# A two-layer decoder trunk on one core: the steps of a large and a small expert in a new order

## The chip, the cores and the metric

The kernel runs on one core of a Trainium2 chip. The metric is the device time of one execution in microseconds (us). Before the change the median of three runs is 1153.97 us (1151.48 to 1154.01).

## The reference, cut to what matters

The program computes two decoder layers on 256 tokens of width 1024, in float32. The change touches the last stage only, a mixture of experts: a router picks two of eight experts for each token, and each expert is a SwiGLU network with 2816 hidden columns.

```
logits = h @ router                       # (256, 8)
top_val, top_idx = top_k(logits, 2)
gates = scatter(softmax(top_val))         # (256, 8), two per row
for e in range(8):
    y = (silu(h @ w_gate[e]) * (h @ w_up[e])) @ w_down[e]
    out = out + gates[:, e:e+1] * y
x = x + out
```

The weights of one expert are three matrices of 1024 x 2816 float32. Over eight experts that is 277 MB, which all comes from HBM once.

## The kernel before, in words

**Experts as large and small.** The router's result sorts the experts by their number of tokens (expert 0 is always put first). Four are "large", with up to 128 token slots, four "small", with up to 64 (`BIG`, `HALFP`). A token reaches its slot by a matmul with a one-hot matrix (`gather_split`, `gather_all`), and an expert's output y goes back to the residual x3 by a matmul with the transposed one-hot (`scatter`, line 1508), whose results VectorE adds with the gate.

**Chunks and units.** Each expert is done in 11 chunks (`FC`) of 256 hidden columns. The weights of a chunk are three units of 1 MB (128 x 2048 float32): the first and the second half of the gate and up product (here gu0 and gu1) and the down product (dn). A chunk takes gu0, gu1, then SiLU and product (`ff_act`, `sm_act`: ScalarE, then VectorE), transposes on TensorE (`ff_tr`, two for a large chunk, `sm_tr`, one for a small), a copy out of PSUM, and dn. Eight experts have 264 units.

**Large work.** For a large expert every operand is the sum of a high and a low part in fp32r: ScalarE writes the high part (`wh`), VectorE the low part (`wl`, line 332 by the helper's line), and `mm3` (lines 515 to 518) multiplies three times. A large unit is 12 matmuls with 128 columns of weights. After the transposes ScalarE writes the high part of the hidden values and VectorE the low part.

**Small work.** A small expert multiplies the float32 unit as it was loaded. Its 64 token slots fill half of the array's columns, so two products run side by side, in the column groups 0 to 63 and 64 to 127 (`sm_gu`, `sm_dn`, lines 1532 and 1555).

**The stream of units.** `Stream` (line 692) loads the units in the order of use with DMAs on SyncE's queue (SP, line 442), each into the next free buffer. There are nine buffers in the long run: five `raw`, one `xres`, one of `xg`, `more` and `fl`. A large unit's buffer is free when its split is done (`make`), a small unit's when its matmuls are done (`done`); the load of the next unit is issued at that place of the program, and SP waits there until the buffer is really free. `ahead(n)` splits the next large unit if fewer than n stand split; there are four pairs of split tiles (`HL`).

**The order before.** `items` alternates large and small chunks, with the small ones four chunks late (`LAG`), so that there are 40 cycles of both, four large chunks alone ahead of them and four small ones behind. Each item runs its gu0, the transposes of the item before, its gu1, and the dn of the item before. A cycle, with L the large and S the small chunk (S' and L' the one before), is thus on TensorE:

```
gu0 L | tr S' | gu1 L | dn S' | gu0 S | tr L | gu1 S | dn L
```

A split is asked for after tr S', after tr L and after gu1 S. What is due once in 11 cycles stands behind the dn: the scatter of the finished expert (`pend`), y's split, one-hots, their transposes, and gathers of later experts. `manual_schedule` keeps each engine's instructions in program order. This part of the program is not ordered by the recorder and its costs, which stop at line 1602.

Of the kernel before, what the change touches and what calls it, by code (L numbers as in the profile page):

```python
# [19 lines left out]
P = 128  # L20
EPS = 1e-6
NEG = -1e30
FC = 11
# [26 lines left out]
HL = 4  # L50
# [3 lines left out]
BIG = 4  # L54
HALFP = 64
LAG = 4
# [337 lines left out]
def kernel(ctx: ExitStack, tc: tile.TileContext, a, out: bass.AP):  # L394
# [32 lines left out]
    def pa():  # L427
        return rec.tile(psp, [P, 512], F32, "ps", 8, name="ps")
# [337 lines left out]
    def ff_gu(st, xs, gu, u, ahead=True):  # L766
        wh, wl = st.next(ahead)
        for b in range(len(xs)):
            for kk in range(4):
                k = 4 * u + kk  # L770
                mm3(gu[b], xs[b][0][:, k, :], xs[b][1][:, k, :], wh[:, kk * 512:(kk + 1) * 512],
                    wl[:, kk * 512:(kk + 1) * 512], k == 0, k == 7)

    def ff_act(gu, scales=None, act=None):
        hs = []
        for b in range(len(gu)):
            si = tw(256)
            hh = tw(256)
            if scales:
                tact(si, gu[b][:, 0:256], AF.Silu, scale=scales[b])  # L780
                V.scalar_tensor_tensor(hh, gu[b][:, 256:512], scales[b], si, op0=OP.mult, op1=OP.mult)
            else:
                (act or tact)(si, gu[b][:, 0:256], AF.Silu)
                V.tensor_tensor(hh, gu[b][:, 256:512], si, OP.mult)
            hs.append(hh)
        return hs

    def ff_tr(hs):
        n = 2 * len(hs) * P
        tp = pa()  # L790
        transposes([h[:, i * P:(i + 1) * P] for i in range(2) for h in hs], tp)
        th, tl = tw(n, dt=F32R), tw(n, dt=F32R)
        S.activation(th, tp[:, :n], AF.Copy)
        V.tensor_tensor(tl, tp[:, :n], th.bitcast(F32), OP.subtract)
        return th, tl

    def ff_dn(st, t, yps, first, last, ahead=True):
        wh, wl = st.next(ahead)
        nb = len(yps)
        order = [(b, i, hf) for b in range(nb) for i in range(2) for hf in range(2)]  # L800
        for b, i, hf in sorted(order, key=lambda o: o[2]) if last else order:
            rec.late = HALF if last and hf else 0
            sl = slice((i * nb + b) * P, (i * nb + b + 1) * P)
            ws = slice(i * 1024 + hf * 512, i * 1024 + (hf + 1) * 512)
            mm3(yps[b][hf], t[0][:, sl], t[1][:, sl], wh[:, ws], wl[:, ws], first and i == 0, last and i == 1)
# [53 lines left out]
    for g in range(2):  # L859
        ps = [pa() for i in range(2)]  # L860
        for u in range(2):
            wh, wl = split(raw0[u]) if g == 0 else unit(a["w0"][2 + u])
            for c in range(4):
                o = ps[c // 2][:, (c % 2) * 256:(c % 2) * 256 + 256]
# [8 lines left out]
        for c in range(4):  # L873
            j = 4 * g + c
# [624 lines left out]
    def y_split(yps):  # L1499
        rec.late = 0  # L1500
        y = [(tw(dt=F32R), tw(dt=F32R)) for i in range(2)]
        for i in range(2):
            rec.late = HALF if i else 0
            S.activation(y[i][0], yps[i], AF.Copy)
            V.tensor_tensor(y[i][1], yps[i], y[i][0].bitcast(F32), OP.subtract)
        return y

    def scatter(t, y, g, acc, store=False):
        for i in range(2):
            rec.late = HALF if i else 0  # L1510
            cs = slice(i * 512, (i + 1) * 512)
            for b in range(2):
                sp = pa()
                T.matmul(sp, t[:, b * P:(b + 1) * P], y[i][0], start=True, stop=False)
                T.matmul(sp, t[:, b * P:(b + 1) * P], y[i][1], start=False, stop=True)
                V.scalar_tensor_tensor(acc[:, b, cs], sp, g(b), acc[:, b, cs], op0=OP.mult, op1=OP.add)
                if store:
                    dma(ov[:, b, cs], acc[:, b, cs])
        rec.late = 0
# [5 lines left out]
    def large_split(src):  # L1525
        x = large_tile()
        S.activation(x[0], src, AF.Copy)
        V.tensor_tensor(x[1], src, x[0].bitcast(F32), OP.subtract)
        return x


    def sm_gu(xs, gu, u):
        w = st.next(False)
        for kk in range(4):
            k = 4 * u + kk
            wv = w[:, kk * 512:(kk + 1) * 512].rearrange("p (g f) -> p g f", g=2)
            for i in range(2):
                mmx(gu[i * HALFP:(i + 1) * HALFP, 0:256].rearrange("p (g f) -> p g f", g=2), xs[:, k],
                    wv[:, :, i * P:(i + 1) * P], k == 0, k == 7)
        st.done()  # L1540

    def sm_act(gu):
        si, hh = tw(P), tw(P)
        tact(si, gu[:, 0:P], AF.Silu)
        V.tensor_tensor(hh, gu[:, P:256], si, OP.mult)
        return hh

    def sm_tr(hh):
        tp = pa()
        transposes([hh], tp)  # L1550
        t = tw(P)
        S.activation(t, tp[:, 0:P], AF.Copy)
        return t
# [14 lines left out]
        return lambda: gtile([P, 2048], F32, n, 2) if n == "xres" else mo([P, 2048], n)  # L1568


    items = []
    for g in range(BIG * FC + LAG):
        if g < BIG * FC:
            items.append((False, *divmod(g, FC)))
        if g >= LAG:
            items.append((True, *divmod(g - LAG, FC)))
    regs = {}

    def source(r, j):

        if r == 0:
            return a["moe"][j]

        def at_run():
            if r not in regs:
                regs[r] = nc.values_load(ids[0:1, r:r + 1], engines=[mybir.EngineType.SP], min_val=0, max_val=7)
            return a["moe"][bass.ds(regs[r] * (3 * FC) + j, 1)].rearrange("u p c -> p (u c)")
        return at_run

    srcs, whole = [], []  # L1590
    for i in range(len(items) + 1):
        for it, js in ((items[i] if i < len(items) else None, (0, 1)), (items[i - 1] if i else None, (2,))):
            for j in js if it else ():
                srcs.append(source(it[1] + (BIG if it[0] else 0), 3 * it[2] + j))
                whole.append(it[0])
    st = Stream(srcs, ([(place("xres"), 999), (place("xg0"), XG)],
                       [(place("xg1"), 999), (place("more"), 999), (place("fl"), 999)]), whole)
    xb = large_tile()
# [6 lines left out]
    xs = top([P, BIG, 8, HALFP], "xs")  # L1605
    oh_s = one_hots(BIG, BIG, HALFP)
    ov = out.rearrange("(b p) d -> p b d", p=P)
    ys, ohs, ohts, hs, pend = {}, {}, {}, {}, None
    N = len(items)
    for i in range(N + 1):  # L1610
        it = items[i] if i < N else None
        was = items[i - 1] if i else None
        alone = not (it and was and it[0] != was[0])
        if it:
            sm, p, c = it
            gu = pa()
            xsp = xs[:, p] if sm else [xb]
            sm_gu(xsp, gu, 0) if sm else ff_gu(st, xsp, [gu], 0, False)
        if was:
            t = sm_tr(hs[was]) if was[0] else ff_tr(hs[was])  # L1620
        st.ahead(HL if alone or it[0] else HL - 1)
        if it:
            sm_gu(xsp, gu, 1) if sm else ff_gu(st, xsp, [gu], 1, False)
            hs[it] = sm_act(gu) if sm else ff_act([gu])
            if not sm and c == FC - 1 and p < BIG - 1:
                xb = large_split(xl[:, p % 2])
        if alone or it[0]:
            st.ahead(HL)
        if was:
            wsm, wp, wc = was  # L1630
            if wc == 0:
                ys[wsm] = [pa(), pa()]
            (sm_dn if wsm else lambda t, y, *f: ff_dn(st, t, [y], *f, False))(t, ys[wsm], wc == 0, wc == FC - 1)
            if alone:
                st.ahead(HL)
        if pend:
            scatter(*pend)
            pend = None
        if was and was[2] == FC - 1:
            r = was[1] + (BIG if was[0] else 0)  # L1640
            pend = (ohts[was[0]], y_split(ys[was[0]]), lambda b, r=r: gateo[:, b, r:r + 1], x3, i == N)
        if not it:
            continue
        if c == 0:
            ohs[sm] = both_halves(BIG + p) if sm else one_hots(p, 1)[:, :, 0]
        if c == 1:
            ohts[sm] = oht_of(ohs[sm][:, 0], ohs[sm][:, 1])
        if sm:
            continue
        if p == 0 and c < LAG:  # L1650
            for k in range(2 * c, 2 * c + 2):
                gather_all(k, oh_s, xs)
        if p == 0 and LAG + 2 <= c < LAG + 6:
            if c == LAG + 2:
                xl, oh_l = mo([P, 2, 8, P], "xg0"), one_hots(1, 2)
            for k in range(2 * (c - LAG - 2), 2 * (c - LAG - 1)):
                gather_all(k, oh_l, xl)
        if p == 1 and 2 <= c < 6:
            if c == 2:
                oh_l = one_hots(3, 1)  # L1660
            for k in range(2 * c - 4, 2 * c - 2):
                gather_all(k, oh_l, xl[:, 0:1])
    scatter(*pend)
    man.close()


# [177 lines left out]
```

## Time and profile before

| what | value |
|---|---|
| median of three runs | 1153.97 us |
| profiled execution | 1151.45 us, span of its instructions 1149.7 us |
| TensorE busy | 1121.7 us (98%) |
| VectorE busy | 713.0 us (62%) |
| ScalarE busy | 588.5 us (51%) |
| read from HBM | 345.95 MB, 302 GB/s over the span |
| mean granted TensorE clock | 0.995 |

The span is the time from the first to the last instruction of the profiled execution. Busy times of TensorE are modelled at the ends of matmuls, so a busy TensorE need not be one at its best pace: the starts of instructions are read here, not their durations. The expert stage goes from about 467 us to the end.

### The profile page before, as it was taken

How to read it: one execution, taken by the hardware profiler on the slowest of the kernel's cores; microseconds unless marked ns; L12 is line 12 of the kernel's file. 1: busy time of each engine (PE TensorE's matmuls, PEld its weight loads, DVE VectorE, ACT ScalarE, POOL GpSimd, SP SyncE). 2: the span in 40 equal slices, each digit the busy share in tenths (PEclk: the TensorE clock that was granted, in tenths of full speed). 3: DMA queues.
4: the chain of work that ended last, by engine and by line, in shares of the span. 5: the costliest groups of instructions: out<-in, count | busy, mean ns of one | idle time of the engine just before them, and what ended most of it. 6: DMA issues, size and time to landing. Idle time of an engine off the chain costs nothing.

```text
span 1149.7 us, 16360 instructions
## 1 busy us (share of the span) xinstructions
PE 1121.7 (98%) x6091; PEld 825.0 (72%) x6091; DVE 713.0 (62%) x1170; ACT 588.5 (51%) x987; POOL 29.0 (3%) x59
## 2 busy tenths in 40 slices
PE   6999999999999999999999999999999999999997
PEld 6888888888877877786766667666666666666663
DVE  5989955445388877785456455557556556565531
ACT  5868744434378656573545444444454444444421
POOL 1040000000300000000000000000000000000000
PEclk9999999999999999899999999999999999999999
DMA  9551565556334515389999999999999999999994
GB/s 351 186 200 74 183 219 184 183 183 202 135 135 181 220 37 186 145 308 376 374 406 419 394 412 384 396 423 422 421 422 421 422 422 420 421 423 419 423 420 161
DMA packets 52070, 348.14 MB, mean 303 GB/s; under 512 B 5904, under 2 KB 6032, under 8 KB 11536
## 3 DMA queue, kind: packets, MB, share of 16 engines
q1 hardware_dynamic: 51984, 347.02, 76.1%
q8 instruction: 50, 0.82, 0.3%
q14 instruction: 36, 0.29, 0.1%
HBM read 345.95 MB, written 1.05 MB: 302 GB/s over the span
## 4 chain that ended last, share of the span: by engine, by line
PE 68%; DMA 19%; DVE 7%; ACT 4%; issue 1%; SPq 0%; ACTq 0%; DVEq 0%
DMA xres<-in_moe_dram 18%; PE ps L516 15%; PE ps L518 15%; PE ps L517 15%; PE ps L332 14%; PE ps L327 10%; DVE wl L332 4%; ACT wh L332 4%; DMA raw<-in_w_dram 1%; DVE wl L327 1%; DVE xres L332 0%; DVE tw L327 0%; DVE tw L332 0%; SPq L446 0%; DVE more L327 0%
## 5 line engine op out<-in xcount | busy, mean ns | idle before, releaser
L332 DVE TENSOR_TENSOR wl<-raw,wh 128x2048 fp32r<-128x2048 f32 x89 | 204.1, 2294 | 153.9 <-ACT wh L332 153.4
L516 PE MATMUL ps<-wh,fh 128*128 128x512 f32 (+2 forms) x720 | 290.3, 403 | 0.0
L517 PE MATMUL ps<-wl,fh 128*128 128x512 f32 (+2 forms) x720 | 279.7, 388 | 0.0
L332 ACT ACTIVATE tw<-ps 128x128 f32<-128x128 f32 (+2 forms) x202 | 72.9, 363 | 320.1 <-PE ps L332 288.6
L332 ACT ACTIVATE wh<-raw 128x2048 fp32r<-128x2048 f32 x89 | 169.9, 1909 | 60.4 <-PE ps L518 56.5
L516 PEld LDWEIGHTS ps<-wh,fh 128*128 128x128 f32 x720 | 135.9, 189 | 28.1
L517 PEld LDWEIGHTS ps<-wl,fh 128*128 128x128 f32 x720 | 136.0, 189 | 23.9
L332 DVE TENSOR_TENSOR tw<-ps,tw 128x256 f32<-128x256 f32 (+3 forms) x158 | 66.7, 427 | 137.1 <-ACT tw L332 136.9
L518 PE MATMUL ps<-wh,fl 128*128 128x512 f32 (+2 forms) x368 | 142.1, 386 | 0.0
L518 PE MATMUL ps<-wh,fh 128*128 128x512 f32 x352 | 138.3, 393 | 0.0
L332 DVE TENSOR_TENSOR wl<-xres,wh 128x2048 fp32r<-128x2048 f32 x39 | 89.2, 2288 | 46.1 <-ACT wh L332 46.1
L332 PE MATMUL ps<-raw,xs 128*64 128x256 f32 x960 | 116.3, 384 | 0.0
L516 PE MATMUL ps<-wh,tw 128*128 128x512 f32 (+1 forms) x276 | 113.7, 412 | 0.7 <-ACT tw L327 0.7
L518 PE MATMUL ps<-wh,tw 128*128 128x512 f32 (+1 forms) x276 | 108.9, 395 | 0.0
L517 PE MATMUL ps<-wl,tw 128*128 128x512 f32 (+1 forms) x276 | 108.7, 394 | 0.0
L332 ACT ACTIVATE wh<-xres 128x2048 fp32r<-128x2048 f32 x39 | 74.8, 1918 | 55.6 <-DMA xres<-in_moe_dram 53.2
L327 DVE TENSOR_TENSOR wl<-raw,wh 128x512 fp32r<-128x512 f32 (+1 forms) x149 | 98.3, 680 | 2.4 <-ACT wh L327 2.4
L332 PEld LDWEIGHTS ps<-raw,xs 128*64 128x64 f32 x960 | 64.8, 137 | 41.3 <-issue 14.5
L327 ACT ACTIVATE wh<-raw 128x512 fp32r<-128x512 f32 (+1 forms) x131 | 75.3, 627 | 16.8 <-PE ps L518 13.2
L518 PEld LDWEIGHTS ps<-wh,fl 128*128 128x128 f32 x368 | 69.1, 188 | 14.6 <-DVE fl L327 0.5
L518 PEld LDWEIGHTS ps<-wh,fh 128*128 128x128 f32 x352 | 66.3, 188 | 14.5
L516 PEld LDWEIGHTS ps<-wh,tw 128*128 128x128 f32 x276 | 51.9, 188 | 26.6 <-issue 15.4
(280 smaller groups left out, 1332.3 us busy)
## 6 DMA issues: line engine op xcount, KB each, us to landing
raw<-in_moe_dram SPq DMA_DIRECT2D x142, 1024.0 KB, 9.4
xres<-in_moe_dram SPq DMA_DIRECT2D x41, 1024.0 KB, 10.5
raw<-in_ffn_dram SPq DMA_DIRECT2D x30, 1024.0 KB, 4.8
xg<-in_moe_dram SPq DMA_DIRECT2D x27, 1024.0 KB, 9.3
more<-in_moe_dram SPq DMA_DIRECT2D x26, 1024.0 KB, 10.8
fl<-in_moe_dram SPq DMA_DIRECT2D x25, 1024.0 KB, 9.7
raw<-in_w_dram SPq DMA_DIRECT2D x23, 1024.0 KB, 4.9
raw<-in_ffn_dram SPq DMA_DIRECT2D x12, 256.0 KB, 3.8
```

The lines of the kernel that those rows point to most:

```text
L327: return (self.name, self.cost(fn, args, kw), lambda: real(*args, **kw))
L332: return getattr(self.eng, fn)(*args, **kw)
L516: nc.tensor.matmul(ps, xh, wh, start=start, stop=False)
L517: nc.tensor.matmul(ps, xh, wl, start=False, stop=False)
L518: nc.tensor.matmul(ps, xl, wh, start=False, stop=stop)
```

## The change

The alternating items become a list of steps. Each step is one unit's matmuls (`gu0`, `gu1`, `dn`), the transposes of a chunk (`tr`), the scatters that are due (`late`), or the rest (one-hots, their transposes, gathers). A full cycle is now, with l0 and s0 the chunks before:

```
tr l0 | gu0 l | late | tr s0 | dn l0 | gu1 l | rest | dn s0 | gu0 s | gu1 s
```

The units are loaded in the order of these steps. After each `tr` and each `dn` the stream is asked for a split up to four. An expert's scatter, which stood behind the next dn, now comes in the next cycle's `late`. The one-hots of an expert are made after its first gu1 and transposed five steps later or at the first `rest` from then on.

```diff
-    items = []
-    for g in range(BIG * FC + LAG):
-        if g < BIG * FC:
-            items.append((False, *divmod(g, FC)))
-        if g >= LAG:
-            items.append((True, *divmod(g - LAG, FC)))
+    def chunk(sm, g):
+        return (sm, *divmod(g, FC)) if 0 <= g < BIG * FC else None
+
+    steps = []
+    for g in range(BIG * FC + LAG + 1):
+        l, l0, s, s0 = chunk(False, g), chunk(False, g - 1), chunk(True, g - LAG), chunk(True, g - LAG - 1)
+        if l and s0:
+            o = [("tr", l0), ("gu0", l), ("late", None), ("tr", s0), ("dn", l0), ("gu1", l), ("rest", l),
+                 ("dn", s0), ("gu0", s), ("gu1", s)]
+        elif l0:
+            o = [("gu0", l), ("tr", l0), ("gu0", s if not l else None), ("tr", s0), ("gu1", l), ("more", l), ("dn", l0),
+                 ("late" if l else "", None), ("rest", l), ("dn", s0), ("gu0", s if l else None), ("gu1", s)]
+        else:
+            o = [("gu0", l or s), ("tr", s0), ("gu1", l or s), ("more", l), ("dn", s0), ("late", None), ("rest", l)]
+        steps += [(k, it) for k, it in o if it or k == "late"]
...
+    unit_of = {"gu0": 0, "gu1": 1, "dn": 2}
+    used = [(k, it) for k, it in steps if k in unit_of]
+    srcs = [source(it[1] + (BIG if it[0] else 0), 3 * it[2] + unit_of[k]) for k, it in used]
+    whole = [it[0] for k, it in used]
...
-    for i in range(N + 1):
-        it = items[i] if i < N else None
-        was = items[i - 1] if i else None
-        alone = not (it and was and it[0] != was[0])
...
+    for n, (k, it) in enumerate(steps):
+        if k == "late":
+            while pend:
+                scatter(*pend.pop(0))
+            continue
+        sm, p, c = it
+        if k == "more":
+            st.ahead(HL)
+        elif k in ("gu0", "gu1"):
+            if k == "gu0":
+                gu[sm] = pa()
+            if sm:
+                sm_gu(xs[:, p], gu[sm], unit_of[k])
+            else:
+                ff_gu(st, [xb], [gu[sm]], unit_of[k], False)
+            if k == "gu1":
+                hs[sm] = sm_act(gu[sm]) if sm else ff_act([gu[sm]])
+                if not sm and c == FC - 1 and p < BIG - 1:
+                    xb = large_split(xl[:, p % 2])
+                if c == 0:
+                    ohs[sm] = n, both_halves(BIG + p) if sm else one_hots(p, 1)[:, :, 0]
+        elif k == "tr":
+            ts[sm] = sm_tr(hs[sm]) if sm else ff_tr(hs[sm])
+            st.ahead(HL)
+        elif k == "dn":
+            if c == 0:
+                ys[sm] = [pa(), pa()]
+            if sm:
+                sm_dn(ts[sm], ys[sm], c == 0, c == FC - 1)
+            else:
+                ff_dn(st, ts[sm], [ys[sm]], c == 0, c == FC - 1, False)
+            st.ahead(HL)
+            if c == FC - 1:
+                r = p + (BIG if sm else 0)
+                pend.append((ohts[sm], y_split(ys[sm]), lambda b, r=r: gateo[:, b, r:r + 1], x3, n == len(steps) - 2))
+        else:
+            for e in list(ohs):
+                if n >= ohs[e][0] + 5:
+                    o = ohs.pop(e)[1]
+                    ohts[e] = oht_of(o[:, 0], o[:, 1])
...
```

The gathers in the last branch are the ones of before, with the same conditions.

## Rows read from the trace of the kernel before

**Rows 1.** The page, busy time, share of the span and instructions of each engine.
```profile
PE 1121.7 (98%) x6091; PEld 825.0 (72%) x6091; DVE 713.0 (62%) x1170; ACT 588.5 (51%) x987; POOL 29.0 (3%) x59
```

**Rows 2.** The page, the chain that ended last, shares of the span by line.
```profile
DMA xres<-in_moe_dram 18%; PE ps L516 15%; PE ps L518 15%; PE ps L517 15%; PE ps L332 14%; PE ps L327 10%; DVE wl L332 4%; ACT wh L332 4%; DMA raw<-in_w_dram 1%; DVE wl L327 1%; DVE xres L332 0%; DVE tw L327 0%; DVE tw L332 0%; SPq L446 0%; DVE more L327 0%
```

**Rows 3.** Windows of the expert stage: busy us, clock, DMA share, GB/s.
```profile
515.00:740.00 225.00, 223.88 (x1236) 149.38 (x1235) 122.19 (x112) 104.35 (x123) 0.00 (x0) 1.00 0.98 392
740.00:1110.00 370.00, 369.83 (x2014) 246.74 (x2013) 213.19 (x188) 169.96 (x183) 0.00 (x0) 1.00 1.01 421
```

**Rows 4.** Waits of TensorE and ScalarE from 740 us: total, times, longest.
```profile
PE ps L332 <- DVE tw L332: 0.2, 1, 0.2
...
ACT wh L332 <- DMA xres<-in_moe_dram: 53.2, 23, 4.0
```

**Rows 5.** Timeline of TensorE, one bare cycle: start, us, engine, line, tiles.
```profile
821.90 1.94 PE L332 MATMUL ps<-raw,tw 128*64 128x512 f32 x8
823.66 1.90 PE L332 MATMUL ps<-xg,xs 128*64 128x256 f32 x16
825.49 0.44 PE L332 MATMUL ps<-cp,tw 128*128 128x128 f32 x2
825.86 1.95 PE L332 MATMUL ps<-raw,xs 128*64 128x256 f32 x16
827.74 0.50 PE L516 MATMUL ps<-wh,tw 128*128 128x512 f32 x1
...
830.65 0.39 PE L516 MATMUL ps<-wh,fh 128*128 128x512 f32 x1
...
836.34 1.94 PE L332 MATMUL ps<-more,tw 128*64 128x512 f32 x8
...
842.18 0.50 PE L516 MATMUL ps<-wh,tw 128*128 128x512 f32 x1
```

**Rows 6.** Timeline of TensorE, two transposes inside 128-column work.
```profile
709.61 0.39 PE L517 MATMUL ps<-wl,tw 128*128 128x512 f32 x1
...
711.94 0.40 PE L518 MATMUL ps<-wh,tw 128*128 128x512 f32 x1
712.17 0.38 PE L332 MATMUL ps<-cp,tw 128*128 128x128 f32 x2
712.31 0.47 PE L516 MATMUL ps<-wh,fh 128*128 128x512 f32 x1
712.62 0.39 PE L517 MATMUL ps<-wl,fh 128*128 128x512 f32 x1
```

**Rows 7.** The chain in order of time: start, us, what.
```profile
755.08 1.93 ACT wh L332
```

**Rows 8.** Timelines of ScalarE and VectorE, [idle before, its releaser].
```profile
829.70 1.92 ACT L332 ACTIVATE wh<-xres 128x2048 fp32r<-128x2048 f32 x1 [1.39 <-DMA xres<-in_moe_dram]
...
1079.01 0.42 DVE L332 TENSOR_TENSOR tw<-ps,tw 128x256 fp32r<-128x256 f32 x1 [2.45 <-ACT tw L332]
...
1083.02 0.28 DVE L332 TENSOR_TENSOR tw<-ps,tw 128x128 f32<-128x128 f32 x1
...
1084.18 1.92 ACT L332 ACTIVATE wh<-xres 128x2048 fp32r<-128x2048 f32 x1 [3.24 <-DMA xres<-in_moe_dram]
...
1086.13 2.29 DVE L332 TENSOR_TENSOR wl<-xres,wh 128x2048 fp32r<-128x2048 f32 x1 [2.83 <-ACT wh L332]
```

**Rows 9.** Timeline of TensorE, small down products on both sides of a cycle with gathers.
```profile
702.24 1.94 PE L332 MATMUL ps<-xg,tw 128*64 128x512 f32 x8
...
718.12 1.94 PE L332 MATMUL ps<-fl,tw 128*64 128x512 f32 x8
```

**Rows 10.** DMA issues in 712 to 732 us: KB each, median us to landing.
```profile
more<-in_moe_dram SPq DMA_DIRECT2D x1, 1024.0 KB, 4.7
```

**Rows 11.** Timeline of TensorE, the last large and the last small down product.
```profile
1109.18 0.50 PE L516 MATMUL ps<-wh,tw 128*128 128x512 f32 x1
...
1137.54 1.94 PE L332 MATMUL ps<-xg,tw 128*64 128x512 f32 x8 [0.37 <-ACT tw L332]
```

More of the change, by code (lines that the diff above doesn't have):

```diff
@@ L1588, in source @@
         return at_run
[L1590 to L1595, printed above, removed]
+    unit_of = {"gu0": 0, "gu1": 1, "dn": 2}
+    used = [(k, it) for k, it in steps if k in unit_of]
+    srcs = [source(it[1] + (BIG if it[0] else 0), 3 * it[2] + unit_of[k]) for k, it in used]
+    whole = [it[0] for k, it in used]
     st = Stream(srcs, ([(place("xres"), 999), (place("xg0"), XG)],
@@ L1607 @@
     ov = out.rearrange("(b p) d -> p b d", p=P)
-    ys, ohs, ohts, hs, pend = {}, {}, {}, {}, None
-    N = len(items)
-    for i in range(N + 1):
-        it = items[i] if i < N else None
-        was = items[i - 1] if i else None
-        alone = not (it and was and it[0] != was[0])
[L1614 to L1627, printed above, removed]
-            st.ahead(HL)
[L1629 to L1662, printed above, removed]
@@ L1663 @@
-    scatter(*pend)
+    gu, hs, ts, ys, ohs, ohts, pend = {}, {}, {}, {}, {}, {}, []
+    for n, (k, it) in enumerate(steps):
[5 more added lines that the diff above has]
+        if k == "more":
+            st.ahead(HL)
+        elif k in ("gu0", "gu1"):
[30 more added lines that the diff above has]
+                    ohts[e] = oht_of(o[:, 0], o[:, 1])
+            if p == 0 and c < LAG:
+                for j in range(2 * c, 2 * c + 2):
+                    gather_all(j, oh_s, xs)
+            if p == 0 and LAG + 2 <= c < LAG + 6:
+                if c == LAG + 2:
+                    xl, oh_l = mo([P, 2, 8, P], "xg0"), one_hots(1, 2)
+                for j in range(2 * (c - LAG - 2), 2 * (c - LAG - 1)):
+                    gather_all(j, oh_l, xl)
+            if p == 1 and 2 <= c < 6:
+                if c == 2:
+                    oh_l = one_hots(3, 1)
+                for j in range(2 * c - 4, 2 * c - 2):
+                    gather_all(j, oh_l, xl[:, 0:1])
```

## The prediction

> **What bounds the kernel now.** I read first the page's shares of busy time [rows 1], then the chain that ended last, by line [rows 2], then two windows of the expert stage [rows 3], then the waits in it [rows 4], and last the timelines of single cycles. The reader is to see two candidates that are both full. TensorE is busy 98% of the span, and in 740 to 1110 us 369.83 of 370 us; in that stage it waits for others 0.2 us in all [rows 1, 3, 4]. The DMA engines are full as well: share 1.01 and 421 GB/s in 740 to 1110, against 0.98 and 392 GB/s in 515 to 740 [rows 3]. The line with most of the chain is a transfer, the load of an expert unit into xres, 18% [rows 2], and ScalarE waits 53.2 us for just these loads [rows 4].
>
> So the stage has two paces. TensorE's: a bare cycle (a large and a small chunk, six units) goes from the small down product at 821.90 to the next at 836.34, 14.44 us [rows 5]. The DMA's: the split of xres starts at 755.08 and at 1084.18, each time on a landing, 22 cycles apart [rows 7, 8]; 329.10 / 22 = 14.96 us, and six units of 1,048,576 bytes in 14.96 us are again 421 GB/s. Cycles with gathers or scatters take TensorE longer, 15.88 us for the one from 702.24 to 718.12 [rows 9]. Up to about 740 us TensorE sets the pace and the DMA waits for free buffers; from there on the DMA has no time left, and TensorE lives on its lead: ScalarE's wait before the xres split, 1.39 us at 829.70, has grown to 3.24 us at 1084.18 [rows 8].
>
> **The change, part by part.**
> (1) *Switches on TensorE.* Before, the two transposes of the large chunk stand between the halves of the small gate and up product. First half 823.66 to 825.49 = 1.83, the transposes to 825.86 = 0.37, second half to 827.74 = 1.88; then the large down product to 830.65 = 2.91 [rows 5]. Inside 128-column work, two transposes and one of the matmuls round them cost 712.62 - 711.94 = 0.68 for two steps of 0.23 and the transposes, so these cost 0.22; and ten steps of a large down product take 711.94 - 709.61 = 2.33, so its twelve without an entry 2.79, and the entry is 2.91 - 2.79 = 0.12 [rows 6]. After, the small block is its down product as before (1.76), the first half 1.76 (an estimate: as the down product, which too is followed by small work), the second half, with its exit, 1.85 (between 1.83 and 1.88). The transposes open the large block, 0.22 + 0.12 = 0.34, and the large down product costs 2.79. Before 1.83 + 0.37 + 1.88 + 2.91 = 6.99; after 1.76 + 1.85 + 0.34 + 2.79 = 6.74. The saving is 0.25 us, a bare cycle 14.19. Bounds: 0.15, if only the transposes gain, and 0.40, with both halves at 1.76 and no entry. I take the sum of the nearest rows, 0.25. For 40 cycles this is 10.0 us, if TensorE alone decided.
>
> (2) *Splits and lead.* In both kernels up to four large units stand split; ScalarE (1.92) and then VectorE (2.29) split each [rows 8], and both work in program order. After the change a split comes behind gu0 L (A), behind dn L (B) and behind dn S (C). Put gu0 L at 0: trS is done at 2.85, dn L 5.64, gu1 L 8.5, dn S 10.25, gu0 S 12.0, gu1 S 13.85, trL 14.19. (Cycles are numbered by their large chunk, 0 to 43; gu0, gu1 and dn are a chunk's three units, tr its transposes.) C splits the gu0 L of the cycle after next, so the 13th unit from the cycle's first must have landed. Behind C in program order stand the small chunk's SiLU and product (0.28 on VectorE) and the large chunk's high and low halves (low 0.42) [rows 8]. If the unit lands at D, the next dn L starts no sooner than D + 1.92 + 2.29 + 0.28 + 0.42 + 0.2 (an estimate for five hops; the one from ScalarE at 1086.10 to VectorE at 1086.13 is 0.03) = D + 5.1. The unit itself is used 14.19 - 2.85 = 11.34 later, so it must land 16.4 us ahead of its use. Before, only a copy and the next split stand behind the late split of xres, and the unit split at 829.70 is used at 842.18 [rows 5, 8], 12.5 us on: TensorE could run closer behind the DMA than the new order lets it.
>
> (3) *Where the DMA then is.* Nine buffers are always held. Releases in a new cycle, from its start: A 2.73 + 4.21 = 6.95, B 9.85, dn S 10.25, C 13.1 (8.5 + 0.4 for the large SiLU, an estimate by the 0.42 above, + 4.21); gu0 S and gu1 S stand behind C on SP's queue, 13.1 and 13.85. The unit that C needs is issued at gu1 S of the cycle before. Take cycle 17, the first bare one after many with extras. Before, its gu0 L starts at 712.31 [rows 6]; the dn L ahead of it, 2.91, now comes behind it, and the blocks of 13 small chunks have gained 13 x 0.25 = 3.25: it starts at 706.15. Cycle 16 lasts 15.88 - 0.25 = 15.63, so its A releases at 697.47. A load that finds the queue empty lands in 4.7 us [rows 10]: 702.17. B's, 2.9 later, lands at 705.07, and the other four at 14.96 / 6 = 2.49 each: 715.03. From here the DMA is never out of work: A of cycle 17 releases at 713.1, and its data flow 4.7 - 2.49 = 2.2 later, about when the last load is done. So 24 cycles on, the same unit of cycle 41 lands at 715.03 + 24 x 14.96 = 1074.1. It is the 245th of 264 in the order of loads; before, the 245th landed at 1084.18 [rows 8].
>
> (4) *The end.* dn L in cycle 42 starts at 1074.1 + 5.1 = 1079.2. Nothing large is left for C, so two cycles run at TensorE's pace: 1079.2 + 14.19 + 14.19 - 2.85 = 1104.7. Then the last trL (0.34) and the work that before went from the last dn L at 1109.18 to the last dn S at 1137.54, 28.36 [rows 11]: that one starts at 1133.4. What follows (y's split, scatter, store) is the same. Gain 4.1 us; with the bounds of (1), over 13 + 3 cycles, 2.5 and 6.5.
>
> (5) *Put at nothing.* The first four large chunks keep their order. Gathers, one-hots, scatters are the same instructions behind other steps; the one-hots' transposes come five steps later, a whole expert ahead of their scatter. A scatter's accumulations now stand on VectorE ahead of A, whose unit has over 20 us to its use. If that cover is gone, each of the six boundaries before cycle 41 costs some 2 us, of which TensorE wins back 14.96 - 14.19 = 0.77 a cycle.
>
> **The sum.** The profiled execution took 1151.45 (span 1149.7); less 4.1 it is 1147.35. It stands 2.5 under the median of the runs, 1153.97, so the forecast for the median is 1153.97 - 4.1 = 1149.9.
>
> **Rivals.**
> *TensorE decides alone.* The transfers keep up and 40 x 0.25 - 0.34 = 9.7 us are won: 1144.3. For it: TensorE's 0.2 us of waits. Against: the rate stayed at 421 GB/s with a share of 1.01 through 370 us [rows 3]; bare cycles of 14.19, or 14.71 with at most 14.96 - 14.44 = 0.52 for boundaries, want 443 to 428 GB/s. [...] The long windows of this trace stop at 421.
> *The lead eats the gain.* The work at boundaries (y's split, that of the next large input) goes through the same two queues as the chain to D + 5.1. If it adds some 3 us to it at the last boundary before cycle 42, about 1 us is left: 1153. For it: the chain has no slack once the DMA leads. Against: five cycles lie between that boundary and cycle 42.
> *Bursts starve the DMA (slower).* While the DMA sets the pace, SP stands at C and then issues three loads at once, at D + 4.2. From D on three units are left in the queue, 7.5 us; the new data flow from D + 4.2 + 2.2 = D + 6.4. The slack is 1.1 us. Against: that is enough by the rows. For: before, releases came more evenly, so no row shows the rate with so short a queue. From 4.1 / 24 = 0.17 us of lost DMA time in a cycle on the change is slower; at 0.4 us it is 9.6 - 4.1 = 5.5 us slower: 1159.5.
> *It doesn't do what it says*: the switches cost the same wherever they stand. Then (3) starts 3.25 later and the gain is under 1 us: 1153, counted with the second rival.
>
> **How the numbers follow.** Forecast 0.50 (own range 1147 to 1152), TensorE alone 0.17, gain eaten 0.18, starved 0.15. A measurement of this kernel can tell some 0.3%, 3.5 us, from no change. Of the forecast's 0.50, 0.30 lies beyond that and 0.20 within. Faster 0.30 + 0.17 = 0.47; same 0.20 + 0.18 = 0.38; slower 0.15. The range begins a little below the first rival and ends on the way into the starved case: 1143 to 1157.
>
> **What would show it.** (1): bare cycles of 14.2 us where TensorE still leads the pace, transposes at 0.3, no step between the small halves. (2), (3): from about 750 us on TensorE waits some 0.7 us a cycle for VectorE's large low half or small product, ScalarE waits for loads more than 53 us, and the rate is 421 GB/s from 700 us on. (4): the last small down product at about 1133, its load long landed. Wrong if TensorE still never waits (the end then comes near 1144), or if the rate in 740 to 1070 falls below 418 GB/s.

## The result and the profile after

The changed kernel is slower: 1170.44 us (median of 5 runs, 1169.43 to 1175.09) against 1153.06 for the kernel before in the same session, a ratio of 1.0164 with a 95% interval of 1.0150 to 1.0178. The forecast was 1149.9. The execution read below took 1169.43, span 1167.7.

Read in the order of the prediction. First the page: busy time of TensorE, then the chain that ended last, by line.

```profile
PE 1115.0 (95%) x6091; PEld 832.0 (71%) x6091; DVE 711.0 (61%) x1170; ACT 591.5 (51%) x987; POOL 29.0 (2%) x59
...
PE ps L332 21%; PE ps L516 17%; PE ps L517 17%; PE ps L518 17%; PE ps L327 10%; DMA raw<-in_moe_dram 5%; ACT wh L332 2%; DMA xres<-in_moe_dram 2%; DVE wl L332 2%; DVE tw L332 1%; DMA raw<-in_w_dram 1%; DVE wl L327 1%; DVE tw L327 0%; DVE xres L332 0%; SPq L446 0%
```

TensorE has less to do, 1115.0 us against 1121.7 [rows 1], and still the span is 18.0 us longer: it waits now. The windows of the expert stage, with the columns of [rows 3] (busy us of five engines, clock, DMA share, GB/s), say that the loads slowed down too, where they had been the limit: 411 GB/s for 421.

```profile
515.00:740.00 225.00, 218.56 (x1232) 152.55 (x1232) 126.00 (x113) 108.65 (x122) 0.00 (x0) 0.98 0.98 398
...
740.00:1110.00 370.00, 353.29 (x1941) 240.51 (x1940) 206.38 (x182) 167.40 (x178) 0.00 (x0) 1.00 1.00 411
```

The waits in the same 370 us (total, times, longest) name what stands in front of TensorE, for 0.2 us before [rows 4]:

```profile
ACT wh L332 <- DMA raw<-in_moe_dram: 66.0, 15, 5.5
...
PE ps L332 <- DVE tw L332: 16.5, 18, 1.9
```

One cycle in time, on SP's queue, ScalarE, VectorE and TensorE (start, us, engine, line, tiles, [idle before, releaser]). C's unit lands and ScalarE starts at 739.05; VectorE's half of the split and the small product follow; the small transposes wait for that.

```profile
736.12 0.33 SPq L442 DMA_DIRECT2D xg<-in_moe_dram  x1
743.32 0.33 SPq L442 DMA_DIRECT2D fl<-in_moe_dram  x1
743.90 7.41 SPq L442 DMA_DIRECT2D raw<-in_moe_dram  x4
...
739.05 1.92 ACT L332 ACTIVATE wh<-fl 128x2048 fp32r<-128x2048 f32 x1 [4.62 <-DMA fl<-in_moe_dram]
...
741.00 2.29 DVE L332 TENSOR_TENSOR wl<-fl,wh 128x2048 fp32r<-128x2048 f32 x1 [5.12 <-ACT wh L332]
743.21 0.61 DVE L332 TENSOR_TENSOR tw<-ps,tw 128x128 f32<-128x128 f32 x2
...
743.55 0.33 PE L332 MATMUL ps<-cp,tw 128*128 128x128 f32 x1 [1.10 <-DVE tw L332]
743.63 0.48 PE L516 MATMUL ps<-wh,tw 128*128 128x512 f32 x1
```

SP issues nothing from 736.12 to 743.32, and then three loads on end, the rest of the x4 from 748 on. Behind such a gap the rate falls, here in windows of 3 us:

```profile
740.00:743.00 3.00, 2.45 (x11) 1.69 (x9) 2.00 (x1) 1.41 (x3) 0.00 (x0) 1.00 1.04 429
743.00:746.00 3.00, 2.45 (x11) 2.05 (x12) 0.82 (x3) 2.08 (x2) 0.00 (x0) 1.00 0.93 328
746.00:749.00 3.00, 3.00 (x14) 2.44 (x14) 2.64 (x2) 1.92 (x1) 0.00 (x0) 1.00 0.99 396
```

The second place is the gathers' one-hots, which the prediction put at nothing. VectorE makes them (tile c against poso) behind a split and the large product; TensorE stands 2.21 us in the middle of its 128-column block, and the small down product behind it takes 3.68 us instead of 1.94. The window of 8 us below it shows why: its granted clock is 0.67, and the loads, whose buffers come free late, fall to 325 GB/s.

```profile
653.88 0.42 DVE L332 TENSOR_TENSOR tw<-ps,tw 128x256 f32<-128x256 f32 x1
654.21 0.48 DVE L332 TENSOR_TENSOR tw<-c,poso 128x128 fp32r<-128x128 f32 x2
...
654.64 0.66 PE L332 MATMUL ps<-tw,xnh 128*128 128x128 f32 x2 [2.21 <-DVE tw L332]
...
656.50 3.68 PE L332 MATMUL ps<-more,tw 128*64 128x512 f32 x8
```

```profile
656.00:664.00 8.00, 8.00 (x43) 3.84 (x42) 2.29 (x1) 2.29 (x3) 0.00 (x0) 0.67 0.83 325
```

The third is the end. In cycle 42 C still finds a large unit to split, the down unit of chunk 43, which is used a whole cycle later. Its split starts on its landing, at 1110.10; TensorE waits 3.03 us and runs the next 5 us at a granted clock of 0.66 (the window behind the rows). The last small down product starts at 1155.82, at 1137.54 before [rows 11].

```profile
1110.10 1.92 ACT L332 ACTIVATE wh<-raw 128x2048 fp32r<-128x2048 f32 x1 [6.55 <-DMA raw<-in_moe_dram]
...
1114.60 0.33 PE L332 MATMUL ps<-cp,tw 128*128 128x128 f32 x1 [3.03 <-DVE tw L332]
...
1155.82 1.94 PE L332 MATMUL ps<-raw,tw 128*64 128x512 f32 x8 [0.37 <-ACT tw L332]
```

```profile
1114.00:1119.00 5.00, 4.40 (x13) 3.48 (x14) 0.87 (x3) 0.28 (x1) 0.00 (x0) 0.66 0.90 349
```

What did come out is the pace where nothing waits. The small block is 811.41 to 816.73, the cycle to the next small down product 14.09 us, for 14.44 before [rows 5]:

```profile
811.41 1.94 PE L332 MATMUL ps<-more,tw 128*64 128x512 f32 x8
813.18 3.62 PE L332 MATMUL ps<-raw,xs 128*64 128x256 f32 x32
816.73 0.44 PE L332 MATMUL ps<-cp,tw 128*128 128x128 f32 x2
...
825.50 1.94 PE L332 MATMUL ps<-xg,tw 128*64 128x512 f32 x8
```

### The profile page after: what moved, and what is told of

It is laid out like the page before. It is cut to its first block, busy times and chain, and to the rows that moved or that the text cites. A ratio compares the mean times of both kernels' runs of the same rounds, so it can differ in the third digit from the quotient of the medians.

```text
span 1167.7 us, 16332 instructions
## 1 busy us (share of the span) xinstructions
PE 1115.0 (95%) x6091; PEld 832.0 (71%) x6091; DVE 711.0 (61%) x1170; ACT 591.5 (51%) x987; POOL 29.0 (2%) x59
## 4 chain that ended last, share of the span: by engine, by line
PE 82%; DMA 7%; DVE 5%; issue 3%; ACT 2%; SPq 0%; DVEq 0%; ACTq 0%
PE ps L332 21%; PE ps L516 17%; PE ps L517 17%; PE ps L518 17%; PE ps L327 10%; DMA raw<-in_moe_dram 5%; ACT wh L332 2%; DMA xres<-in_moe_dram 2%; DVE wl L332 2%; DVE tw L332 1%; DMA raw<-in_w_dram 1%; DVE wl L327 1%; DVE tw L327 0%; DVE xres L332 0%; SPq L446 0%
## 5 line engine op out<-in xcount | busy, mean ns | idle before, releaser
L332 DVE TENSOR_TENSOR wl<-raw,wh 128x2048 fp32r<-128x2048 f32 x136 | 311.9, 2294 | 273.8 <-ACT wh L332 273.3
L332 ACT ACTIVATE wh<-raw 128x2048 fp32r<-128x2048 f32 x136 | 260.1, 1914 | 176.0 <-DMA raw<-in_moe_dram 92.5
L332 ACT ACTIVATE tw<-ps 128x256 fp32r<-128x256 f32 (+3 forms) x202 | 69.2, 362 | 246.0 <-PE ps L332 198.7
L332 DVE TENSOR_TENSOR tw<-ps,tw 128x256 f32<-128x256 f32 (+3 forms) x158 | 63.6, 425 | 68.2 <-ACT tw L332 68.1
L332 PE MATMUL ps<-raw,xs 128*64 128x256 f32 x832 | 98.1, 381 | 0.0
L332 PEld LDWEIGHTS ps<-raw,xs 128*64 128x64 f32 x832 | 59.8, 138 | 41.4 <-issue 14.4
L516 PEld LDWEIGHTS ps<-wh,tw 128*128 128x128 f32 x276 | 53.8, 195 | 13.6 <-ACT tw L327 0.9
L518 PEld LDWEIGHTS ps<-wh,tw 128*128 128x128 f32 x276 | 52.7, 191 | 12.9 <-DVE tw L327 0.4
L332 PE MATMUL ps<-cp,tw 128*128 128x128 f32 x188 | 41.4, 292 | 19.8 <-DVE tw L332 19.8
```

Of the source, the lines that this page charges most:

```text
L332: return getattr(self.eng, fn)(*args, **kw)
L516: nc.tensor.matmul(ps, xh, wh, start=start, stop=False)
L518: nc.tensor.matmul(ps, xl, wh, start=False, stop=stop)
```

## The experiments

Three theories. *Loads* (in the expectations "burst"): SP stands at C's reload, the loads of gu0 S and gu1 S queue behind it, and the DMA idles once a cycle. *Chain*: C's place among the steps costs TensorE the time by itself, through the queues of ScalarE and VectorE. *One-hots*: the two stalls and the clock behind them. Ratios are to the kernel before, with 95% intervals.

**C later.** The small down step splits nothing; the next large transposes do.

```
             if sm:
                 sm_dn(...)
             else:
                 ff_dn(...)
-            st.ahead(HL)
+                st.ahead(HL)
```

> The changed kernel, but the third split of a cycle (C) is not asked for behind dn S; it moves to the next request, behind the large chunk's transposes, and so stands behind the small product and the large halves on ScalarE and VectorE, and behind the two small releases on SP's queue. Theory chain (C waits for its landing and holds up what stands behind it on three queues): most of the loss goes, TensorE's waits fall from 26 us to under 8, 1156 us (the one-hot stalls stay). Theory one-hots (the loss is the two stalls of TensorE on one-hots and the half clock behind them): 1168 us, no change. Both put the loads of the DMA-bound stage at 421 GB/s at best.

Measured 1162.57, 1.0085 (1.0064 to 1.0107): 7.9 less than the changed kernel, in between. TensorE's waits for VectorE's tw fall from 26.1 to 10.4 us, the two one-hot stalls of 2.34 and 2.21 included; others come at the boundaries, where an expert is finished and its scatter is due (5.6 for xres), and the clock falls behind both one-hot stalls (0.98 over 515 to 740 us): the small product at 547.43 takes 3.44 us, the one at 660.37 3.61 (first a row of the waits, then one of TensorE's timeline). The edit also orders the loads anew and takes the last large split out of cycle 42, so alone it decides nothing.

```profile
PE ps L516 <- DVE xres L332: 5.6, 3, 1.9
```

```profile
547.43 3.44 PE L332 MATMUL ps<-xg,tw 128*64 128x512 f32 x8
```

**One-hots a cycle earlier.**

```
-                    xl, oh_l = mo([P, 2, 8, P], "xg0"), one_hots(1, 2)
+                    xl = mo([P, 2, 8, P], "xg0")
...
-                if c == 2:
-                    oh_l = one_hots(3, 1)
...
+            if (p, c) == (0, LAG + 1):
+                oh_l = one_hots(1, 2)
+            if (p, c) == (1, 1):
+                oh_l = one_hots(3, 1)
```

> The changed kernel, but the one-hots of the two gathers are made one cycle earlier, so that no gather waits for them in mid-block. Theory chain: only the two stalls of 2.4 and 2.2 us and the half clock behind the second go, 6 to 8 us in all where TensorE sets the pace, part of it lost again to the DMA: 1164 us. Theory one-hots: nearly all of the loss goes, 1155 us.

Measured 1166.93, 1.0125 (1.0094 to 1.0156): 3.5 less than the changed kernel. Both stalls are gone, the waits behind C are not. So the stalls are at most a small part by themselves: the intervals of the two kernels overlap (1.0150 to 1.0178 for the changed one), so by the times alone this gain is hardly clear of noise. The row of the waits:

```profile
PE ps L332 <- DVE tw L332: 25.4, 26, 3.0
```

**Loads first.** C stays where it is on ScalarE and VectorE; the reload of its buffer alone is issued later, behind the loads for gu0 S and gu1 S.

```
-            st.ahead(HL)                  # behind dn L and dn S
+            if st.ready < HL:
+                st.make(sm)               # split; behind dn S the freed buffer is kept back
...
                 hs[it] = sm_act(gu[sm]) if sm else ff_act([gu[sm]])
+                if sm:
+                    st.pay()              # now load into it
```

> The changed kernel with C in its place on ScalarE and VectorE, but the buffer that it frees is reloaded last, behind gu0 S and gu1 S, so that SP does not stand at C with two free buffers behind it. Theory chain in the form that the engines' order counts: TensorE goes on waiting for the small product, 20 us or more, 1166 to 1170 us. Theory burst (only SP's order counts, the DMA runs dry because three loads come at once): the rate in 740 to 1110 rises from 411 to 420 GB/s and the time falls to 1158 us.

Measured 1160.19, 1.0065 (1.0046 to 1.0084): 10.3 less. SP now issues two loads at 737.70 and 739.43, where it stood before; the dip at 743 is gone, and the long window is back at 420 GB/s, although C and the waits behind it stay (18.8 us with the two one-hot stalls). *Loads* is right about the rate, *chain* wrong: it had TensorE lose as much with C in place. SP's timeline, and two windows:

```profile
736.17 0.33 SPq L442 DMA_DIRECT2D xg<-in_moe_dram  x1
737.70 0.33 SPq L442 DMA_DIRECT2D raw<-in_moe_dram  x1
739.43 0.33 SPq L442 DMA_DIRECT2D xres<-in_moe_dram  x1
743.22 8.01 SPq L442 DMA_DIRECT2D raw<-in_moe_dram  x3
```

```profile
743.00:746.00 3.00, 2.55 (x12) 2.10 (x13) 0.79 (x4) 2.08 (x2) 0.00 (x0) 1.00 0.98 410
...
740.00:1090.00 350.00, 339.79 (x1874) 231.88 (x1874) 201.46 (x179) 163.98 (x176) 0.00 (x0) 1.00 1.01 420
```

**C later and one-hots earlier** (the first two edits).

> Both edits, C behind the large halves and the one-hots a cycle early. Theory chain: the two add up, 1148 to 1150 us, so faster than the kernel before; the DMA sets the pace at 421 GB/s from about 700 us on. If the gain of the new order is not real on TensorE: 1153 us or more.

Measured 1155.24, 1.0024 (1.0011 to 1.0036): missed, it is not faster than before. The loads run at 410 GB/s in 740 to 1090 us; no run here shows why. At three boundaries a scatter's additions to xres now stand behind the moved split on VectorE, TensorE waits for them (a row of its timeline), and its clock falls, to 0.66 in the stretch round that row (a window).

```profile
972.41 0.79 PE L516 MATMUL ps<-wh,tw 128*128 128x512 f32 x1 [1.87 <-DVE xres L332]
```

```profile
970.00:980.00 10.00, 8.13 (x24) 6.08 (x23) 7.93 (x7) 3.77 (x2) 0.00 (x0) 0.66 1.02 422
```

**Loads first and one-hots earlier.**

> The two edits together: the loads of gu0 S and gu1 S are issued ahead of the reload of C's buffer, and the one-hots of the two gathers are made a cycle earlier. If the edits add up (the one-hots cost 3.5 us of 1170.4, the loads 10.3), 1156.5. If each also takes away what sets the other off (a stall lets the clock fall, TensorE releases tiles late, the DMA idles), less than the sum: 1152 to 1155, 412 GB/s or more in 515 to 740 and 420 in 740 to 1090. If the DMA alone sets the time once it runs at 420 GB/s, a TensorE that is further ahead buys nothing: 1159 to 1160.

Measured 1152.99, 1.0009 (0.9995 to 1.0023), no difference from before and 17.5 less than the changed kernel, where the parts sum to 13.8. The times of the one-hots' run spread too far (1162.90 to 1169.60) to show by themselves that the two edits help each other. The loads of the stage before 740 us show it better: 416 GB/s here (the window), against 398 in the changed kernel, 402 with the loads first and 406 with the one-hots earlier.

```profile
515.00:740.00 225.00, 222.92 (x1267) 157.26 (x1266) 131.16 (x118) 113.91 (x127) 0.00 (x0) 1.00 1.00 416
```

**The same, and the end mended**: C of cycle 42 leaves the last down unit to the next split.

```
+    last = max(j for j, (k, it) in enumerate(used) if not it[0] and k != "dn")
...
-            if st.ready < HL:
+            if st.ready < HL and not (sm and len(st.made) > last):
```

> As the run with both edits, and C of cycle 42 leaves the down unit of large chunk 43 alone, so that it is split at the next opportunity, behind the next 128-column transposes. If taking that unit five units ahead is what cost the end (TensorE waits 3.0 us for the small transposes, then runs at the lower clock for some 5 us: 3.0 + 1.7, and a little behind it), 4 to 5 us less than the run with both edits, so 1149 to 1152, not slower than the kernel before. If the landing of that last large unit sets the end in any case, no gain: within 1 us of the run with both edits.

Measured 1146.47 (1145.69 to 1146.76), 0.9950 (0.9936 to 0.9963): faster than both kernels, and 6.5 less than without the last edit, where 4 to 5 were expected. C's units of cycles 17 and 41 land at 714.76 and 1074.74, and the last small down product starts at 1132.98. A window of the stage, then rows of the timelines of ScalarE and TensorE:

```profile
740.00:1090.00 350.00, 340.87 (x1896) 232.07 (x1897) 200.49 (x178) 161.87 (x172) 0.00 (x0) 1.00 1.01 420
```

```profile
714.76 1.91 ACT L332 ACTIVATE wh<-raw 128x2048 fp32r<-128x2048 f32 x1 [3.47 <-DMA raw<-in_moe_dram]
...
1074.74 1.91 ACT L332 ACTIVATE wh<-raw 128x2048 fp32r<-128x2048 f32 x1 [4.13 <-DMA raw<-in_moe_dram]
...
1132.98 1.94 PE L332 MATMUL ps<-raw,tw 128*64 128x512 f32 x8 [0.37 <-ACT tw L332]
```

**The end alone**, on the changed kernel.

> The changed kernel with that one edit: C of cycle 42 leaves the down unit of large chunk 43 alone. By the same theory 4 to 5 us less than the changed kernel (1170.4), so 1165.5 to 1166.5, the last small down product some 4.5 us earlier than 1155.8, no stall over 1 us at 1114. If the landing sets the end, 1170.

Measured 1164.61, 1.0103 (1.0085 to 1.0121): 5.8 less. The last large unit is split no earlier (1113.19; this execution, at 1167.54 the slowest of its four, was 3.1 us behind the changed kernel's by the unit of cycle 41), yet no transposes wait for it, and the last small down product is at 1154.12, 1.7 us earlier where 4.5 were expected. Rows of ScalarE's and TensorE's timelines:

```profile
1113.19 1.92 ACT L332 ACTIVATE wh<-raw 128x2048 fp32r<-128x2048 f32 x1 [0.84 <-DMA raw<-in_moe_dram]
...
1154.12 1.94 PE L332 MATMUL ps<-raw,tw 128*64 128x512 f32 x8 [0.37 <-ACT tw L332]
```

**Both kernels with fewer loads.** One unit in six of a full cycle, the small experts' down unit, isn't in the list of loads; its products read another tile, so the results mean nothing. TensorE then sets the pace.

```
-        w = st.next(False)                         # sm_dn
+        w = xs.rearrange("p b k n -> p (b k n)")
...
-        st.done()
```

> The kernel before without the loads of the small experts' down units (one load in six of a full cycle): their products read a tile that is in SBUF anyway, so the products stay and their numbers mean nothing. The DMA then has 12.5 us of work per cycle at 421 GB/s against 14.4 of TensorE's, so TensorE sets the pace. All theories: bare cycles of 14.44 or a little less up to the end, 1145 to 1151. If TensorE waited for the loads nowhere before (its waits are 0.2 us), the gain over 1152 is only what the end gives, 0 to 4 us.

> The changed kernel without the same loads. If what it lost was the loads' order alone (units that land late, C started late), then with units that land early C starts at once, the transposes behind it don't wait, bare cycles take 14.09 throughout, and the time is 6 to 12 us less than that of the kernel before with the same loads left out (27 bare cycles by 0.35, eight of gathers by 0.3 to 0.7, less some 4 to 7 for the one-hots' two stalls). If C's place itself costs TensorE the time (the transposes of the next block stand behind it on VectorE), the waits of 0.5 to 3 us remain and it is not faster, or slower.

Measured 1150.55, 0.9985 (0.9975 to 0.9995), for the kernel before, and 1141.36, 0.9912 (0.9893 to 0.9930), for the changed one: 9.2 us apart, in the changed one's favour. TensorE's timeline, first two rows of the kernel before (14.44 us apart), then three of the changed one (14.10 apart; its one-hots still stall) and a row of its waits: 4.6 us in two, which are the one-hots, are all that TensorE waits there for VectorE's tw.

```profile
821.67 1.94 PE L332 MATMUL ps<-xs,tw 128*64 128x512 f32 x8
...
836.11 1.94 PE L332 MATMUL ps<-xs,tw 128*64 128x512 f32 x8
```

```profile
545.31 0.71 PE L332 MATMUL ps<-tw,xnh 128*128 128x256 f32 x2 [2.35 <-DVE tw L332]
...
805.55 1.94 PE L332 MATMUL ps<-xs,tw 128*64 128x512 f32 x8
...
819.65 1.94 PE L332 MATMUL ps<-xs,tw 128*64 128x512 f32 x8
```

```profile
PE ps L332 <- DVE tw L332: 4.6, 2, 2.4
```

With units that land early, TensorE waits for VectorE nowhere behind C in its new place. *Chain* falls here a second time.

## Why the prediction was wrong

The sum ran over three dates: when C's unit of cycle 18 lands (715.03 + 14.96), the pace over the 23 cycles to the unit of cycle 41, and the stretch from there to the last small down product. The same dates of the profiled executions, in us:

| | cycle 18 | per cycle | cycle 41 | from there | last dn S |
|---|---|---|---|---|---|
| forecast | 729.99 | 14.96 | 1074.1 | 59.3 | 1133.4 |
| changed kernel | 739.05 | 15.38 | 1092.77 | 63.05 | 1155.82 |
| one-hots earlier | 736.96 | 15.36 | 1090.20 | 61.51 | 1151.71 |
| loads first | 738.95 | 15.01 | 1084.24 | 63.05 | 1147.29 |
| end alone | 737.77 | 15.57 | 1095.86 | 58.26 | 1154.12 |
| loads, one-hots | 729.80 | 15.01 | 1075.12 | 64.48 | 1139.60 |
| all three | 729.64 | 15.00 | 1074.74 | 58.24 | 1132.98 |

The changed kernel's 22.4 us on the forecast's last date are 9.1 by cycle 18, 23 x 0.42 = 9.6 after it and 3.7 at the end. The end alone mends the stretch from cycle 41, the loads first the pace; the first date takes the loads and the one-hots together. With all three, every date lies within 1.1 us of the forecast's, so the pace and the end were reckoned soundly, and three premises weren't. (The median there, 1146.47, still lies under the forecast of 1149.9: the forecast added 2.5 us from the profiled execution to the median, and with all three the profiled execution is the median.)

The first date agrees in part by luck. (3) built it on TensorE, whose gu0 L of cycle 17 was to start at 706.15, with a DMA that waits for free buffers until then. With all three that product starts at 702.2, 3.9 us earlier, and the unit lands at 714.76, 12.5 us behind it and not 8.9: the loads run at 416 GB/s from 515 to 650 us and 417 from 650 to 740, shares 1.00 and 1.01, where the kernel before has 390 and 395, 0.98 in both. ScalarE waits 3.47 us for that unit; the kernel before has no wait of ScalarE for a load in 515 to 740. The DMA sets the pace sooner than put, and the two misses cancel.

(3) failed first: "From here the DMA is never out of work". The price was written in the third rival: SP stands at C, 0.4 us a cycle would make it slower. That is the number measured (15.38 - 14.96 = 0.42), but it had a chance of 0.15, because a slack of 1.1 us by the rows seemed enough. The loads did come where I put them, 743.32 - 739.05 = 4.27 after D, and of the three loads left in the queue the last landed at D + 7.4 (10.3 us after its issue at 736.12), as put. The rate still fell to 328 GB/s for 3 us.

Half-microsecond windows of the changed kernel place the fall: 410 GB/s to 744.5, then 180, 229 and 360, and 393 from 746.0 on. Over the 21 cycles from 739.05 to 1092.77 in which C waits over 2.5 us for its load, the mean is 420 GB/s up to D + 4.5, lowest, 372 and 377, from D + 5.5 to D + 6.5, and 406 to 423 in the 2 us behind. So the new data came at about D + 6.4, as put, and the term that failed is the queue's 7.5 us: three loads that have landed by then did not keep the rate up until then, and the slack of 1.1 us, counted in landings, was none. The 9.1 us of the first date are not this premise's alone: either the loads or the one-hots mended move it by 2.1 us at most, both together by 9.3.

(5) failed: "Put at nothing. ... one-hots ... are the same instructions behind other steps". They are, but in `rest` they now stand behind a split and the large product on VectorE with TensorE waiting in mid-block, and TensorE pays 2.2 to 2.4 us of stall each time and, behind the second, 3.68 us for the small down product, which took 1.94 behind the first.

(4) failed in a detail of the planner: "Nothing large is left for C". One unit was left, the down unit of chunk 43. It cost 5.8 us in the runs by itself, and 6.5 on top of the other two edits.

(2) was right: the large down product behind C starts at D + 4.6 (743.63 - 739.05), put at D + 5.1, and TensorE waits for it. (1) was right in kind and too small: 14.44 - 14.09 = 0.35 us, inside the bounds of 0.15 to 0.40. The exit that I charged to the second small half (1.85) isn't there; the block is 5.32 and not 5.37, and the large block gives the other 0.05.

The rival *TensorE alone* had the rate as its condition. With all three edits the rate is 420 GB/s at a share of 1.01, so DMA sets the pace there too. No window of 350 us or more here shows more than 421, and bare cycles of 14.19 us want 443, six units in each. Only with fewer loads does TensorE's saving show, 9.2 us.

## What to carry to other kernels

When loads are issued in program order from one queue, a step that frees a buffer late must not stand ahead of loads whose buffers are already free (here that order cost 10.3 us): list the issues with their gaps, and trust no slack that is under one load (1.1 us of 2.49 was none here). A reordering that shortens the busiest engine is worth what the other full resource lets through (9.2 us here once a cycle's loads were five for six), so mend that first. And ask of every instruction moved "at nothing" not whether it costs more, but who now waits for it and what stands ahead of it.

## What the hardware showed

I had not expected TensorE's clock to fall behind stalls this short. After stalls of 2.21 us (654.64) and 3.03 us (1114.60) the granted clock of the next stretch was 0.67 (656 to 664) and 0.66 (1114 to 1119): the small down product at 656.50 took 3.68 us for 1.94, and from 1115.58 on large matmuls started 0.43 us apart for 0.23; after one of 2.37 us at 545.77 in the same kernel the small down product took its usual 1.94 us at a clock of 1.00 (547 to 555), while with C moved later a like stall (2.34 us) was followed by one of 3.44 us. In these traces the length of a stall doesn't tell which is followed by the drop: in the changed kernel one of 1.94 us (943.54), shorter than that of 2.37, is followed by a granted clock of 0.67 (943 to 948). The stall of 2.37 us and the product behind it:

```profile
545.77 0.63 PE L332 MATMUL ps<-tw,xnh 128*128 128x256 f32 x2 [2.37 <-DVE tw L332]
...
547.05 1.94 PE L332 MATMUL ps<-xg,tw 128*64 128x512 f32 x8
```
